# A layer with routed experts on one core: a multiplication moved to GpSimd, a third of the one-hot rows moved to VectorE, and the last block's stages scheduled earlier

## The chip, the core and the metric

The kernel runs on one core of a Trainium2 chip. The metric is device time in microseconds, the median of several executions. One execution is also profiled; the time of every instruction below comes from that one. PE is the TensorE matmul engine, DVE the VectorE, ACT the ScalarE, POOL the GpSimd, SP the SyncE, which issues most transfers.

## What is computed

One layer on 512 tokens of width 1024, all in float32: a norm and an input projection; eight heads of latent attention and eight heads of a chunked recurrence (RWKV-7); an output projection added to the input; then a layer of retrieved experts. That last part matters here:

```
q = (h @ w_pq) per head, two halves; s = q . sub_keys
s1, i1 = top_k(first half, 16);  s2, i2 = top_k(second half, 16)
top_s, pos = top_k(s1 + s2 over the 16 x 16 pairs, 16);  idx = i1 * 128 + i2 at pos
gate = softmax(top_s)
act = gelu(sum_d expert_u[idx] * h)
out += sum_k gate * act * expert_v[idx]        # 8 heads x 16 experts for each token
```

There are 128 x 128 = 16,384 experts, each a row of 1024 numbers in `expert_u` and in `expert_v`.

## The kernel before

The tokens are four blocks of 128. Each block passes through stages, written as generators: F (norm and projections of the recurrence, `front`), R (`chunks`), M (attention, `latent`), S (`scan`), B (output projection, norm, retrieval, `back`), and for the two dense blocks T (`routes`). B of block 3 also routes it. A loop at the end of the function picks, stage by stage, which generator emits its next piece, by a planner's estimate of costs.

The order in which instructions are emitted gives each a priority, earlier ones first. A scheduler then builds one fixed order for every engine's queue from these priorities and from its own model of durations; the chip follows this order, each queue strictly in turn. An instruction emitted inside `tc.high_priority(offset=4000)` counts as if it had been emitted 4000 instructions earlier. Before the change, only three helpers of the recurrence use it.

The experts are computed in two ways.

*Gathered rows*, for blocks 0 and 3 (`experts`): for each of the 128 picks of a token, POOL issues an indirect transfer of 128 rows from `expert_u` (L996), DVE multiplies it with h and sums (L1006); later the same for `expert_v`, which DVE adds into `acc` with the weight of each token (L1009). This makes 512 transfers of 128 x 1024 floats into four buffers (six in the early part). They are emitted after the stages, 96 steps of block 0 before the dense part and the rest after it, so the scheduler uses them to fill what is free.

*Dense*, for blocks 1 and 2 (`dense`): all 16,384 experts are computed for all 256 tokens, 128 groups of 128 experts. `up` multiplies a group of `expert_u` with h and applies gelu; `down` multiplies the result with the routing weights and with the group of `expert_v`, into four accumulators in PSUM. Most groups are split into a high and a low half first (L1094 on ACT, L1095 on DVE) and go as three products of halves.

The routing weights of the dense blocks are a matrix of tokens by experts, built by `make_gates` in 32 groups of eight tokens. `slots` holds, for each token (a column) and pick (a partition), the first index, the second index and the gate. For a group, B[pick, token, i] is 1 where i is the first index (L1061, DVE), times the gate (L1062, DVE); A[pick, token, j] is 1 where j is the second index, made on ACT as relu(1 - |j - index|) by eight Abs and one Relu (L1065, L1066). PE multiplies A and B token by token (L1074), and ACT evicts the products into `held` and `away` (L1077, L1078). B has two buffers, A has two, and the products have four banks of PSUM, which become the accumulators of `down` afterwards. The `away` part goes to DRAM and comes back later (L1080). The first 28 groups of `up` (L1133) are emitted before and between the groups of `make_gates`. Block 3's retrieval (L844, its top-16 lists L822 to L830) and routing share this stretch, since nothing in the dense part waits for them but the space they occupy.

Of the kernel before, what the change touches and what calls it, by code (L numbers as in the profile page):

```python
# [2 lines left out]

# [10 lines left out]
AF = mybir.ActivationFunctionType  # L14
OP = mybir.AluOpType
# [3 lines left out]
P = 128  # L19
D = 1024  # L20
S = 512
NB = S // P
# [8 lines left out]
URGENT = 4000  # L31
# [58 lines left out]
def layer_kernel(ctx: ExitStack, tc: tile.TileContext, x, pos, cvec, rvec, w_mla, w_rwkv, w_uq, w_ukv, lora, g2,  # L90
# [20 lines left out]
    mm, act, V, G = nc.tensor.matmul, nc.scalar.activation, nc.vector, nc.gpsimd  # L111
# [26 lines left out]
    def cst(shape, name, dt=F32, pool=pre):  # L138
        return pool.tile(shape, dt, name=name)
# [108 lines left out]
    iotap = cst([P, P], "iotap", pool=con)  # L248
# [14 lines left out]
    for j in range(16):  # L263
# [5 lines left out]
                    op=OP.mult)  # L269
# [26 lines left out]
    def bc(ap, n):  # L296
        return ap[:, :, None].to_broadcast([ap.shape[0], ap.shape[1], n])

    def bm(ap, n):
        return ap[:, None, :].to_broadcast([ap.shape[0], n, ap.shape[1]])  # L300
# [755 lines left out]
    def make_gates(dn, psd, held, far):  # L1056

        i1T, i2T, gT = slots
        for t0 in range(0, nd, 8):
            B = dn.tile([P, D], F32, tag="x", name=f"B{t0}", bufs=XB).rearrange("p (a b) -> p a b", a=8)  # L1060
            V.tensor_tensor(B, bm(iotap, 8), bc(i1T[:, t0:t0 + 8], P), op=OP.is_equal)  # L1061
            V.tensor_tensor(B, B, bc(gT[:, t0:t0 + 8], P), op=OP.mult)  # L1062
            A = dn.tile([P, 8, P], F32, tag="A", name=f"A{t0}", bufs=2)
            for j in range(8):
                act(A[:, j, :], iotap, AF.Abs, scale=-1.0, bias=i2T[:, t0 + j:t0 + j + 1])  # L1065
            act(A, A, AF.Relu, scale=-1.0, bias=1.0)  # L1066
            i = t0 % 16
            if i == 0:
                away = dn.tile([P, D], F32, tag="v", name=f"away{t0}", bufs=VB)
                away = away.rearrange("p (s t i) -> p s t i", s=P // SUB - HELD, i=SUB)  # L1070
            for h in range(2):
                p = psd.tile([P, 512], F32, tag="po", name=f"pg{t0}{h}", bufs=2 * len(DENSE))
                for j in range(4):
                    mm(p[:, j * P:(j + 1) * P], A[:, 4 * h + j, :], B[:, 4 * h + j, :], start=True, stop=True)  # L1074
                p4 = p.rearrange("p (t s i) -> p s t i", t=4, i=SUB)
                t = t0 + 4 * h
                act(held[:, :, t:t + 4, :], p4[:, :HELD], AF.Copy)  # L1077
                act(away[:, :, t % 16:t % 16 + 4, :], p4[:, HELD:], AF.Copy)  # L1078
            if i:
                nc.sync.dma_start(far[:, t0 // 16], away)  # L1080
            yield

    def dense():
# [110 lines left out]
        for i, _ in enumerate(make_gates(dn, psd, held, far)):  # L1194
            for e in range(FIRST + i * rest // n, FIRST + (i + 1) * rest // n):
                up(e, e >= AHEAD)
# [30 lines left out]
    running = [None] * len(lanes)  # L1227
    while any(lanes):
        best = None
        for i, todo in enumerate(lanes):  # L1230
            if not todo:
                continue
            t = at[i]
            if running[i] is None:
                deps = [d for b in todo[0][1] for d in after[todo[0][0]](b) if d[1] >= 0]
                if any(d not in done for d in deps):
                    continue
                t = max([t] + [done[d] for d in deps])
            if best is None or t < best[0]:
                best = (t, i)  # L1240
        t, i = best
        n, bs = lanes[i][0]
        fn, count, cost = stages[n]
        if running[i] is None:
            running[i] = fn(bs) if n == "B" else fn(*bs)
            at[i] = t
        lane[0] = LANE[n]
        try:
            next(running[i])
            at[i] += cost / count  # L1250
        except StopIteration:
            for b in bs:
                done[n, b] = at[i]
            lanes[i].pop(0)
            running[i] = None
# [67 lines left out]
```

## Time and profile before

| | |
|---|---|
| median of 3 executions | 1761.57 us (1759.91 to 1781.8) |
| the profiled execution | 1773.46 us, its span 1771.7 us |
| PE matmul, weight load | 1556.0 us (88%), 1319.3 us (74%) |
| DVE | 1358.6 us (77%) |
| ACT | 808.1 us (46%) |
| POOL | 777.8 us (44%), 512 of its instructions are gathers |
| moved by DMA | 537.52 MB, 303 GB/s; of it by the gathers 268.47 MB |
| mean granted TensorE clock | 0.926 of full speed |

The shares are averages over the whole span; the stages differ in what limits them. A window of the trace gives the busy time of each engine in one stretch, the granted clock, the mean busy share of the 16 DMA engines and the rate. Grouped lines give the work of one source line: how many instructions, how long in total, the mean, then how long the engine stood idle just before them and what ended that.

### The profile page before, as it was taken

How to read it: one execution, taken by the hardware profiler on the slowest of the kernel's cores; microseconds unless marked ns; L12 is line 12 of the kernel's file. 1: busy time of each engine (PE TensorE's matmuls, PEld its weight loads, DVE VectorE, ACT ScalarE, POOL GpSimd, SP SyncE). 2: the span in 40 equal slices, each digit the busy share in tenths (PEclk: the TensorE clock that was granted, in tenths of full speed). 3: DMA queues.
4: the chain of work that ended last, by engine and by line, in shares of the span. 5: the costliest groups of instructions: out<-in, count | busy, mean ns of one | idle time of the engine just before them, and what ended most of it. 6: DMA issues, size and time to landing. Idle time of an engine off the chain costs nothing. (4 is left out here: it accounts for less than half of the span.)

```text
span 1771.7 us, 29597 instructions
## 1 busy us (share of the span) xinstructions
PE 1556.0 (88%) x10803; PEld 1319.3 (74%) x10803; DVE 1358.6 (77%) x2788; ACT 808.1 (46%) x2007; POOL 777.8 (44%) x560
## 2 busy tenths in 40 slices
PE   7999998998799897789995668999969999899992
PEld 6896797876575686569985436788868888888872
DVE  3422435678886689988999857898879899898896
ACT  5645634455423422237798302444425444344440
POOL 1001100546674644454437644454445365464574
PEclk9999998998669889899997889999989999999997
DMA  8545644798889889889996899899999999999997
GB/s 279 187 140 189 228 160 129 273 362 275 300 303 385 297 312 322 311 319 359 377 308 209 314 318 347 335 360 345 350 324 367 347 334 364 348 350 364 331 340 274
DMA packets 165617, 537.52 MB, mean 303 GB/s; under 512 B 17824, under 2 KB 32800, under 8 KB 165472
## 3 DMA queue, kind: packets, MB, share of 16 engines
q0 software_dynamic: 73728, 268.47, 42.4%
q1 hardware_dynamic: 91744, 267.17, 42.2%
q8 instruction: 85, 1.39, 0.3%
q14 instruction: 60, 0.49, 0.1%
HBM read 517.34 MB, written 18.22 MB: 302 GB/s over the span
## 5 line engine op out<-in xcount | busy, mean ns | idle before, releaser
L996 POOL DMA_INDIRECT ga<-in_expert_v_dram,idx x235 | 375.8, 1599 | 315.5 <-DVE acc L1009 205.6
L996 POOL DMA_INDIRECT ga<-in_expert_u_dram,idx x225 | 287.5, 1278 | 312.8 <-DVE ga L1006 244.2
L1009 DVE SCALAR_TENSOR_TENSOR acc<-ga,dots,acc 128x1024 f32<-128x1024 f32 x235 | 300.5, 1279 | 33.3 <-DMA ga<-in_expert_v_dram,idx 32.8
L1006 DVE SCALAR_TENSOR_TENSOR ga<-ga,h 128x1024 f32<-128x1024 f32 x225 | 273.6, 1219 | 29.8 <-DMA ga<-in_expert_u_dram,idx 29.1
L1147 PE MATMUL ps<-dh,uh 128*128 128x256 f32 x800 | 231.7, 290 | 24.8 <-ACT uh L1094 24.8
L1147 PE MATMUL ps<-dh,ul 128*128 128x256 f32 x800 | 231.9, 290 | 13.4 <-DVE ul L1095 13.4
L1147 PE MATMUL ps<-dl,uh 128*128 128x256 f32 x800 | 230.5, 288 | 0.0
L1185 PE MATMUL po<-xh,t 128*128 128x512 f32 x544 | 186.1, 402 | 16.1 <-ACT xh L1094 16.1
L1147 PEld LDWEIGHTS ps<-dh,uh 128*128 128x128 f32 x800 | 157.0, 196 | 32.1 <-ACT uh L1094 27.4
L1147 PEld LDWEIGHTS ps<-dh,ul 128*128 128x128 f32 x800 | 156.7, 196 | 19.6 <-DVE ul L1095 17.1
L1147 PEld LDWEIGHTS ps<-dl,uh 128*128 128x128 f32 x800 | 156.8, 196 | 3.1 <-issue 0.5
L1185 PE MATMUL po<-x2h,t 128*128 128x512 f32 x408 | 135.3, 392 | 2.0 <-ACT x2h L1094 2.0
L1094 ACT ACTIVATE xh<-v 128x1024 fp32r<-128x1024 f32 x68 | 71.9, 1057 | 136.3 <-DMA v<-in_expert_v_dram 61.7
L1095 DVE TENSOR_TENSOR ul<-u,uh 128x1024 fp32r<-128x1024 f32 x100 | 121.9, 1220 | 13.6 <-ACT uh L1094 13.5
L1185 PEld LDWEIGHTS po<-xh,t 128*128 128x128 f32 x544 | 101.8, 192 | 39.6 <-ACT xh L1094 19.5
L844 PE MATMUL ps<-h2T,wst 128*128 128x128 f32 (+1 forms) x768 | 125.2, 319 | 4.2 <-DMA wst<-in_w_pq_dram 2.9
L1094 ACT ACTIVATE uh<-u 128x1024 fp32r<-128x1024 f32 x100 | 104.8, 1051 | 43.2 <-DMA u<-in_expert_ut_dram 33.2
L844 PEld LDWEIGHTS ps<-h2T,wst 128*128 128x128 f32 x768 | 110.8, 197 | 12.8 <-DMA wst<-in_w_pq_dram 2.2
L353 PE MATMUL ps<-hT,wst 128*128 128x129 f32 x896 | 110.8, 277 | 0.6 <-ACT t L311 0.6
L1185 PE MATMUL po<-xl,t 128*128 128x512 f32 x272 | 109.8, 404 | 0.7 <-DVE xl L1095 0.5
L1133 PE MATMUL ps<-t,u 128*128 128x256 f32 x448 | 108.0, 395 | 2.7 <-DMA u<-in_expert_ut_dram 2.0
L353 PEld LDWEIGHTS ps<-hT,wst 128*128 128x128 f32 x896 | 105.3, 191 | 6.3 <-issue 1.3
(423 smaller groups left out, 3132.6 us busy)
## 6 DMA issues: line engine op xcount, KB each, us to landing
u<-in_expert_ut_dram SPq DMA_DIRECT2D x128, 512.0 KB, 6.8
v<-in_expert_v_dram SPq DMA_DIRECT2D x128, 512.0 KB, 6.1
wst<-in_w_rwkv_dram SPq DMA_DIRECT2D x56, 512.0 KB, 4.4
wst<-in_w_pq_dram SPq DMA_DIRECT2D x48, 512.0 KB, 6.6
wst<-in_w_o_dram SPq DMA_DIRECT2D x24, 512.0 KB, 6.2
far<-away SPq DMA_DIRECT2D x16, 512.0 KB, 6.1
G<-far SPq DMA_DIRECT2D x16, 512.0 KB, 12.0
wst<-in_w_mla_dram SPq DMA_DIRECT2D x16, 336.0 KB, 6.5
```

What stands on the lines that cost most here:

```text
L353: mm(p[:, :P + 1], w[:, kc, :], hT[:, kc, :], start=kc == 0, stop=kc == KC - 1)
L844: mm(p[:, :nb * P], w[:, kc, :], h2T[:, kc, :], start=kc == 0, stop=kc == KC - 1)
L996: G.indirect_dma_start(out=t, out_offset=None, in_=table, in_offset=bass.IndirectOffsetOnAxis(ap=idx[:, j:j + 1], axis=0))
L1006: V.scalar_tensor_tensor(u, u, 1.0, h2, op0=OP.mult, op1=OP.mult, accum_out=dots[:, j:j + 1])
L1009: V.scalar_tensor_tensor(acc, row_of(expert_v, j), dots[:, j:j + 1], acc, op0=OP.mult, op1=OP.add)
L1094: act(hi, t, AF.Copy)
L1095: V.tensor_tensor(lo, t, hi, op=OP.subtract)
L1133: mm(p, u[:, kc, :], hd[kc // 2][:, kc % 2, :], start=kc == 0, stop=kc == KC - 1)
L1147: mm(p, a[:, k, :], h[:, kc, :], start=kc + i == 0, stop=kc == KC - 1 and i == 2)
L1185: mm(po[i][n], ww[:, i * P:(i + 1) * P], vv[:, cols], start=e + k == 0, stop=e == P - 1 and k == 2)
```

## The change

It has three parts. In `make_gates` the multiplication of B with the gate is issued on GpSimd instead of VectorE. Of each three groups the third gets its A from one comparison on VectorE instead of the nine operations on ScalarE; that is ten of the 32. And block 3's stages M, S and B are emitted inside `tc.high_priority(offset=4000)`.

```
-            V.tensor_tensor(B, B, bc(gT[:, t0:t0 + 8], P), op=OP.mult)
+            G.tensor_tensor(B, B, bc(gT[:, t0:t0 + 8], P), op=OP.mult)
             A = dn.tile([P, 8, P], F32, tag="A", name=f"A{t0}", bufs=2)
-            for j in range(8):
-                act(A[:, j, :], iotap, AF.Abs, scale=-1.0, bias=i2T[:, t0 + j:t0 + j + 1])
-            act(A, A, AF.Relu, scale=-1.0, bias=1.0)
+            if t0 // 8 % 3 == 2:
+                V.tensor_tensor(A, bm(iotap, 8), bc(i2T[:, t0:t0 + 8], P), op=OP.is_equal)
+            else:
+                for j in range(8):
+                    act(A[:, j, :], iotap, AF.Abs, scale=-1.0, bias=i2T[:, t0 + j:t0 + j + 1])
+                act(A, A, AF.Relu, scale=-1.0, bias=1.0)
...
         try:
-            next(running[i])
+
+            with tc.high_priority(offset=URGENT) if bs == (NB - 1,) and n in "MSB" else nullcontext():
+                next(running[i])
             at[i] += cost / count
```

## Rows read from the trace of the kernel before

**Rows 1.** Windows: stretch, its length, busy us (instructions) by engine, clock, DMA share, GB/s.

```profile
core 0: us, PE busy (x) PEld busy (x) DVE busy (x) ACT busy (x) POOL busy (x), PEclk, DMA share, GB/s
...
700.00:792.00 92.00, 69.27 (x313) 50.41 (x313) 85.09 (x363) 20.61 (x53) 44.90 (x36) 0.87 0.87 316
792.00:989.00 197.00, 174.17 (x1178) 161.32 (x1176) 184.85 (x395) 162.78 (x472) 99.52 (x59) 0.93 0.88 313
989.00:1050.00 61.00, 33.91 (x82) 18.51 (x83) 40.08 (x68) 7.45 (x13) 28.83 (x17) 0.80 0.89 322
1050.00:1742.00 692.00, 639.97 (x3771) 557.82 (x3770) 611.00 (x778) 288.46 (x428) 352.85 (x231) 0.97 0.95 346
1742.00:1771.70 29.70, 0.43 (x2) 0.00 (x0) 16.67 (x16) 0.00 (x0) 10.65 (x9) 0.57 0.71 244
```

**Rows 2.** The last link of the chain of waits: start, duration, what.

```profile
1766.50 1.28 DVE acc L1009
```

**Rows 3.** Groups of ACT, 792 to 989 us: count, busy, mean ns, idle before.

```profile
L1065 ACT ACTIVATE A<-iotap,slots 128x128 f32<-128x128 f32 x256 | 78.9, 406 | 0.0
L1066 ACT ACTIVATE A<-A 128x1024 f32<-128x1024 f32 x32 | 33.9, 1064 | 0.1
...
L1077 ACT ACTIVATE G<-pg 128x256 f32<-128x256 f32 x64 | 24.6, 384 | 19.5 <-PE pg L1074 19.5
```

**Rows 4.** Groups of PE, 792 to 989 us.

```profile
L1074 PE MATMUL pg<-B,A 128*128 128x128 f32 x512 | 71.7, 298 | 10.3 <-DVE B L1062 4.3 <-ACT A L1066 4.0 <-DVE B L1061 2.1
...
L844 PE MATMUL ps<-h2T,wst 128*128 128x128 f32 x256 | 30.9, 275 | 0.0
```

**Rows 5.** Groups of DVE, 792 to 989 us.

```profile
L1009 DVE SCALAR_TENSOR_TENSOR acc<-ga,dots,acc 128x1024 f32<-128x1024 f32 x44 | 56.1, 1274 | 2.9 <-DMA ga<-in_expert_v_dram,idx 2.9
...
L1062 DVE TENSOR_TENSOR B<-B,slots 128x1024 f32<-128x1024 f32 x32 | 38.7, 1213 | 0.1
L1006 DVE SCALAR_TENSOR_TENSOR ga<-ga,h 128x1024 f32<-128x1024 f32 x15 | 18.3, 1218 | 2.2 <-DMA ga<-in_expert_u_dram,idx 2.1
...
L830 DVE FIND_INDEX8 ti<-tv,t 128x8 uint32<-128x128 f32 x16 | 4.4, 285 | 0.0
...
L822 DVE MAX8 tv<-t 128x8 f32<-128x128 f32 x16 | 3.5, 278 | 0.0
```

**Rows 6.** B's comparison by line: min/median/max ns, first and last start.

```profile
L1061 DVE TENSOR_TENSOR B<-iotap,slots x32: 1198/1212/1237, 791.8 to 981.3; 128x1024 f32<-128x1024 f32 x32
```

**Rows 7.** GpSimd's memsets by line, the same columns.

```profile
L616 POOL MEMSET t<- x8: 515/532/544, 42.5 to 467.5; 64x512 f32 x8
```

**Rows 8.** Groups of POOL, 792 to 989 us.

```profile
L996 POOL DMA_INDIRECT ga<-in_expert_v_dram,idx x46 | 83.4, 1813 | 76.0 <-DVE acc L1009 47.2 <-DVE ga L1006 4.8 <-DVE ti L877 3.6
L996 POOL DMA_INDIRECT ga<-in_expert_u_dram,idx x13 | 16.1, 1239 | 20.9 <-DVE ga L1006 9.2 <-DVE ti L824 4.7 <-DMA ga<-in_expert_v_dram,idx 3.4
```

**Rows 9.** Waits, 792 to 989 us: total us, times, longest.

```profile
POOL ga L996 <- DVE acc L1009: 47.2, 28, 4.9
```

**Rows 10.** A power of 128x1 on POOL by line: min/median/max ns.

```profile
L306 POOL TENSOR_TENSOR nfr<-nfv,mhalf x4: 557/990/1475, 192.6 to 774.4; 128x1 f32<-128x1 f32 x4
```

**Rows 11.** POOL in order of time: start, duration, what.

```profile
575.37 1.48 POOL L306 TENSOR_TENSOR nfr<-nfv,mhalf 128x1 f32<-128x1 f32 x1 [3.00 <-DVE nfv L304]
...
990.96 10.59 POOL L996 DMA_INDIRECT ga<-in_expert_u_dram,idx  x1 [0.65 <-DVE acc L1009]
```

**Rows 12.** DVE in order of time, beside these.

```profile
575.20 1.21 DVE L1006 SCALAR_TENSOR_TENSOR gx<-gx,h 128x1024 f32<-128x1024 f32 x1
...
993.62 3.08 DVE L1164 TENSOR_TENSOR wst<-wst,G 128x256 f32<-128x256 f32 x6
```

**Rows 13.** By line from 700 us on: block 3's output projection, its retrieval; slots.

```profile
L787 PE MATMUL ps<-wst,yT x32: 592/592/697, 727.0 to 769.2; 128*128 128x512 f32 x32
...
L844 PE MATMUL ps<-h2T,wst x256: 272/275/275, 799.2 to 879.4; 128*128 128x128 f32 x128
...
L978 ACT ACTIVATE slots<-ps x6: 257/275/283, 772.9 to 793.8; 128x128 f32<-128x128 f32 x6
```

**Rows 14.** Waits of SP's queue, 700 to 1050 us: total us, times, longest.

```profile
SPq L293 <- PE ps L844: 24.2, 10, 4.1
```

More of the change, by code (lines that the diff above doesn't have):

```diff
@@ L1 @@
 import math
-from contextlib import ExitStack
+from contextlib import ExitStack, nullcontext
 import concourse.bass as bass
```

## The prediction

> **What bounds the kernel now.** I read the stage table first [rows 1]: busy time of each engine between the points where the work changes. The reader should see three regimes. From 792 to 989 us the routing matrix is built: DVE is busy 184.85 of 197 us, PE 174.17, ACT 162.78. From 1050 to 1742 us the dense pass runs: the DMA engines are busy 0.95 of the time at 346 GB/s, PE 639.97 of 692 us. Between them lies a hole (989 to 1050) in which PE works 33.91 of 61 us. PE has nothing left after 1742 us (0.43 us), and the chain of waits ends in an accumulation of a gathered row at 1766.5 us [rows 2]. So the dense pass and the gathered rows share the DMA engines to the end, and every gather put off from an earlier stage is paid there: a gather moves 128 rows of 1024 floats, 0.524 MB, which is 1.5 us at 346 GB/s.
>
> Then the groups inside the build. On ACT the Abs, the Relu and two groups of evictions of about 24.6 us each are nearly all of the work, and ACT's largest idle time, 19.5 us, is for products of PE [rows 3]; PE's products wait 10.3 us for A and B [rows 4]. ACT with that wait is 182 of 197 us: the loop through ACT paces the build. DVE is as full, but 74.4 us of it (56.1 + 18.3) are gathered rows, which nothing in the build waits for [rows 5]. Thus less work on ACT shortens the build; less on DVE mainly makes room for gathers.
>
> **The change, part by part.** *The multiplication leaves DVE*: 32 of 1.213 us, 38.7 us [rows 5]. *The one-hot rows of ten groups* (2, 5, ... 29 of 32) go from ACT to DVE: ACT loses 10/32 of 78.9 + 33.9 = 35.3 us [rows 3], DVE gains ten comparisons of B's shape, 10 x 1.212 = 12.1 us [rows 6]. DVE: -26.6 us.
>
> *The multiplication on GpSimd*, 128x1024, has no row. Nearest is a memset that writes 512 columns in 0.532 us [rows 7]: 1.06 us for 1024 if its reads hide behind its writes, 3.2 us if two reads and a write go one after the other. I take the middle, 2.1 us: 67 us on POOL beside 99.5 us of gather issues [rows 8], 167 of 197 us. The Trainium skill (GPSIMD Engine Reference, 3.1) states 4497 ns for an addition twice as wide; an estimate from it is 2.25 us, 72 us in all, and the sum would not move.
>
> The multiplication now stands in POOL's order behind gathers that wait for a buffer, up to 4.9 us each [rows 9]; behind it wait the next gather and the products of its group. B has two buffers and a group takes 197/32 = 6.2 us; comparison, multiplication and products need 1.2 + 2.1 + 2.2 us (71.7/32, [rows 4]), which leaves 6.9 us of 12.3. So I cost this wait at nothing; without that cover, one late multiplication of 10 us costs some 3 us.
>
> *What the multiplication costs DVE* is the disputed term. GpSimd's tiny operation takes 0.56 us at best and 1.48 us when it starts inside a gathered-row instruction of DVE, ending about 0.4 us after that one [rows 10 to 12]. A gather issue stood 10.59 us while DVE ran short two-input instructions with no gap [rows 11, 12]. So DVE makes GpSimd wait. The reverse shows nowhere, but GpSimd read at most 8 columns at a time in this kernel. The hold on DVE is between 0 and the whole multiplication, at most 3.2 us; the rows show DVE keeping its place, so I take 0.6 us, 19 us in all. DVE's net is -7 us.
>
> *The build after that*: ACT 127 us, or 147 with its wait for products; DVE without gathers 184.85 - 74.4 - 7 = 103; PE still 174. PE is next in line, so the build ends 197 - 174 = 23 us earlier. In those 23 us 23/197 x 59 = 7 gathers [rows 8] are not issued and come later, 7 x 1.5 = 10.6 us. Net -12.4 us.
>
> *Block 3's last stages* (attention, scan, output projection, retrieval, routing) go 4000 instructions forward. Before, block 3's output projection ran within 727 to 769 us and its retrieval matmuls at 799 to 879 us, while the dense blocks' lists (slots) were complete at 794 us [rows 13]. So block 3 was behind the dense blocks' routing and beside the build. Put ahead, it takes out of the build 30.9 us of PE [rows 4] and on DVE five groups of list operations (4.4 to 3.5 us, 20 us) and smaller ones, some 30 us [rows 5]. With these go its SyncE loads (8 of w_o, 16 of w_pq, 4 of keys), past the dense blocks' loads and the first expert loads; the weight queue already waited 24.2 us for block 3's matmuls to free a buffer [rows 14]. On POOL its small powers (0.56 to 2.5 us each) pass gathers. What it pays depends on where it lands. PE was idle 22.73 us of 700 to 792: at best it fills that. At worst the dense blocks' routing, and the build with it, starts later by all 30.9 us of PE and gets nothing back. Taken work out of one stage and put into the stage before it, with idle time for most of it and a chain in front that waits for it: I take 0 and keep -22.7 and +30.9 for the range.
>
> **Sum.** The profiled execution took 1773.5 us (span 1771.7), 11.9 above the median of 1761.6. 1773.5 - 12.4 = 1761.1; against the median, 1749 us. This case alone spans 1739 (no gather put off) to 1762 (all of it paid back). A difference under 2%, 35 us, can't be told from none here: below 1726 is faster, above 1797 slower.
>
> **Rivals.**
>
> *The hold (slower).* Place: 792 to 989 us, DVE. If the multiplication keeps DVE out for its whole length, 32 x 2.1 = 67 us come against 26.6 saved: +40.6, of which DVE's 12.2 us of idle time take some. 28.4 us remain, 23 gathered rows of 1.25 us, put off at 1.5 us each: +35, 1797 us; at 3.2 us each, +77, 1838. It costs from a hold of (26.6 + 12.2)/32 = 1.2 us on, and passes 2% at 2.1 us. For: both sides stay nearly full, and POOL waits for DVE in the rows. Against: B's 32 comparisons, in a stretch where POOL is busy half of the time, all last 1198 to 1237 ns [rows 6].
> The Trainium skill (SBUF — State Buffer, "Who interferes with whom") says that a VectorE instruction with two SBUF inputs and a GpSimd instruction that reads SBUF exclude each other for the whole instruction, whichever started first. By that rule this rival decides. The trace agrees for one direction (1.48 against 0.56 us); no run here yet shows the other.
>
> *Block 3 fills the holes (faster).* With its lists done early, 22.7 us of PE's idle time before 792 go: 12.4 + 22.7 = 35, 1726 us. If the space that block 3's pools hold is free early enough for the dense pass to start without the hole of 989 to 1050 (27.1 us of PE idle), 1699. Middle: 1713 us. For: PE idles in both places. Against: in both the DMA engines are at 0.87 and 0.89, so there is little room to load ahead.
>
> *Paid back, or no effect.* Every us won in the build returns as gathers on the DMA engines, and block 3's stages can't move because their tiles wait for block 2's: 1762 us. For: the dense pass at 0.95.
>
> **Chances and range.** Forecast 0.38, paid back 0.17, holes filled 0.25, hold 0.20. Below 1726: 0.20 of the third and 0.06 of the first's tail together with block 3's gain, 0.26. Above 1797: 0.12 of the hold, 0.05 for block 3 delaying the build, 0.17. Between: 0.57. Range 1702 to 1800: the deep end of the holes (under 0.1) and the upper half of the hold (about 0.1) are left out.
>
> **What would show it.** After the change the 32 multiplications stand on POOL at 1.06 to 3.2 us; longer means that they wait inside. DVE's two-input instructions beside them at 1.2 us and without gaps: no hold; gaps of 1 to 2 us in front of them, named after nothing or POOL: hold. ACT in the build about 127 us, the build some 174 us long with PE as its fullest engine. Gathers before the dense pass fewer by about 7, dense pass at 346 GB/s as before. Block 3's retrieval matmuls before the slots are written, and the slots no later than 794 us: step right; slots at 815 or later: block 3 delays the build. Wrong altogether I would be if the dense pass itself changed its length by more than 20 us, since nothing in my sum acts there except gathers.

## The result, and the profile after

The changed kernel takes 1795.0 us (median of 4 runs), the kernel before 1763.5 in the same comparison. The ratio is 1.0137, 95% interval 1.009 to 1.0183; this ratio and those below are taken over the fast runs of each comparison and need not be the quotient of the two medians, which is 1.0179 here. The loss is clear of its interval, but under the 2% from which the prediction would have called the kernel slower. The forecast of 1749 us had the wrong sign; that 1795 lies inside the range of 1702 to 1800 is no merit of the sum, which had the kernel 12 us faster. The profiled execution took 1795.96 us, its span is 1794.2.

The stage table of the changed kernel, as in [rows 1], cut where its own build begins and ends:

```profile
core 0: us, PE busy (x) PEld busy (x) DVE busy (x) ACT busy (x) POOL busy (x), PEclk, DMA share, GB/s
700.00:810.00 110.00, 81.64 (x383) 60.53 (x382) 94.56 (x377) 26.84 (x68) 52.05 (x44) 0.83 0.87 312
810.00:1023.00 213.00, 181.87 (x1172) 167.54 (x1172) 197.57 (x359) 133.89 (x385) 143.32 (x84) 0.90 0.78 272
1023.00:1050.00 27.00, 12.97 (x33) 7.36 (x32) 21.39 (x40) 5.87 (x10) 7.22 (x6) 0.70 0.88 320
1050.00:1775.00 725.00, 670.78 (x3829) 577.20 (x3828) 630.99 (x803) 289.96 (x430) 352.42 (x240) 0.97 0.94 343
1775.00:1794.20 19.20, 0.99 (x5) 0.46 (x3) 11.32 (x12) 0.00 (x0) 4.67 (x4) 0.66 0.71 254
```

Read by the first comparison of B, the last product of a one-hot pair and the last matmul, the two spans divide like this:

| us | before | after | difference |
|---|---|---|---|
| build begins | 791.8 | 809.6 | +17.8 |
| build | 196.5 | 212.1 | +15.6 |
| dense pass to its last matmul | 754.1 | 754.3 | +0.2 |
| tail behind it | 29.3 | 18.2 | -11.1 |

So the run lost 33 us ahead of the dense pass and got 11 back in the tail. ACT did lose its work, 162.8 to 133.9 us, and nothing became shorter for it.

The groups of the changed kernel between 810 and 1023 us, DVE, ACT, PE and POOL (count, busy, mean ns, idle before), answering to [rows 3 to 6] and [rows 8]:

```profile
L1009 DVE SCALAR_TENSOR_TENSOR acc<-ga,dots,acc 128x1024 f32<-128x1024 f32 x41 | 75.9, 1851 | 5.3 <-DMA ga<-in_expert_v_dram,idx 5.1
L1061 DVE TENSOR_TENSOR B<-iotap,slots 128x1024 f32<-128x1024 f32 x32 | 45.1, 1414 | 1.2 <-PE ps L958 1.0 <-PE pg L1077 0.2
L1006 DVE SCALAR_TENSOR_TENSOR ga<-ga,h 128x1024 f32<-128x1024 f32 x11 | 18.9, 1723 | 6.1 <-DMA ga<-in_expert_u_dram,idx 6.1
L1065 DVE TENSOR_TENSOR A<-iotap,slots 128x1024 f32<-128x1024 f32 x10 | 13.8, 1382 | 0.0
...
L1080 ACT ACTIVATE G<-pg 128x256 f32<-128x256 f32 x64 | 24.7, 386 | 45.2 <-PE pg L1077 45.0
...
L1077 PE MATMUL pg<-B,A 128*128 128x128 f32 x512 | 76.0, 307 | 18.3 <-POOL B L1062 16.8 <-ACT A L1069 1.5
...
L1062 POOL TENSOR_TENSOR B<-B,slots 128x1024 f32<-128x1024 f32 x32 | 74.4, 2330 | 24.3 <-DVE B L1061 24.1
```

The means of DVE are the finding. A gathered row's accumulation takes 1851 ns instead of 1274, its dot product 1723 instead of 1218, a comparison 1414 instead of 1212. Without these three lines and the multiplication DVE's busy time in its build was 184.4 - 74.4 - 38.8 - 38.7 = 32.5 us before and is 197.6 - 94.8 - 45.1 - 13.8 = 43.9 now, for 265 small operations instead of 272. Stretching in all: 41 x 0.577 + 11 x 0.505 + 32 x 0.202 + 10 x 0.17 + 11.4 = 48.8 us, 1.5 us for each of the 32 multiplications. Where it lies shows in order of time (start, duration; POOL and DVE of the changed kernel, 857 to 873 us):

```profile
857.71 1.89 POOL L1062 TENSOR_TENSOR B<-B,slots 128x1024 f32<-128x1024 f32 x1 [0.53 <-DVE B L1061]
857.82 2.87 DVE L1009 SCALAR_TENSOR_TENSOR acc<-ga,dots,acc 128x1024 f32<-128x1024 f32 x1
...
862.70 2.02 POOL L1062 TENSOR_TENSOR B<-B,slots 128x1024 f32<-128x1024 f32 x1
...
863.26 1.50 DVE L1015 TENSOR_TENSOR dots<-dots,gate 128x32 f32<-128x32 f32 x1 [0.30 <-ACT dots L1014]
...
866.77 2.01 POOL L1062 TENSOR_TENSOR B<-B,slots 128x1024 f32<-128x1024 f32 x1
866.95 5.55 DVE L1009 SCALAR_TENSOR_TENSOR acc<-ga,dots,acc 128x1024 f32<-128x1024 f32 x3
```

Each of these stretched DVE instructions begins just behind the start of a multiplication and ends after it: 2.87 us begun at 857.82 ends 1.1 us after POOL at 859.60, so its own 1.27 us were hardly begun while POOL worked. A product of 128x32 takes 1.50 us. The wait is inside the instruction; no gap and no wait's name shows it.

Block 3's part shows in the line that writes the dense blocks' lists, at 793.8 us before [rows 13]:

```profile
L978 ACT ACTIVATE slots<-ps x6: 272/282/296, 797.2 to 815.8; 128x128 f32<-128x128 f32 x6
```

### The profile page after: what moved, and what is told of

The parts are those of the page before. It is cut to its first block, busy times and chain, and to the rows that moved or that the text cites. A ratio compares the mean times of both kernels' runs of the same rounds, so it can differ in the third digit from the quotient of the medians.

```text
span 1794.2 us, 29558 instructions
## 1 busy us (share of the span) xinstructions
PE 1583.2 (88%) x10803; PEld 1336.5 (74%) x10803; DVE 1383.5 (77%) x2766; ACT 780.7 (44%) x1919; POOL 811.7 (45%) x592
## 4 chain that ended last, share of the span: by engine, by line
PE 41%; issue 17%; DVE 14%; DMA 14%; POOL 10%; ACT 2%; SPq 0%; POOLq 0%; DVEq 0%; ACTq 0%
POOL ga L996 9%; PE po L1188 7%; PE ps L1150 7%; DMA ga<-in_expert_v_dram,idx 5%; PE ps L353 5%; PE ps L844 4%; DVE acc L1009 4%; DMA ga<-in_expert_u_dram,idx 3%; PE ps L669 3%; DVE ga L1006 2%; DMA v<-in_expert_v_dram 2%; PE ps L787 2%; PE ps L364 1%; DVE B L1061 1%; PE ps L1136 1%
## 5 line engine op out<-in xcount | busy, mean ns | idle before, releaser
L996 POOL DMA_INDIRECT ga<-in_expert_v_dram,idx x235 | 350.6, 1492 | 350.5 <-DVE acc L1009 223.1
L996 POOL DMA_INDIRECT ga<-in_expert_u_dram,idx x225 | 273.4, 1215 | 256.0 <-DVE ga L1006 182.3
L1009 DVE SCALAR_TENSOR_TENSOR acc<-ga,dots,acc 128x1024 f32<-128x1024 f32 x235 | 324.4, 1380 | 31.5 <-DMA ga<-in_expert_v_dram,idx 30.7
L1006 DVE SCALAR_TENSOR_TENSOR ga<-ga,h 128x1024 f32<-128x1024 f32 x225 | 279.0, 1244 | 46.0 <-DMA ga<-in_expert_u_dram,idx 45.7
L1150 PEld LDWEIGHTS ps<-dh,ul 128*128 128x128 f32 x800 | 160.3, 201 | 15.6 <-DVE ul L1098 13.5
L1097 ACT ACTIVATE xh<-v 128x1024 fp32r<-128x1024 f32 x68 | 72.0, 1058 | 120.4 <-DMA v<-in_expert_v_dram 58.7
L1097 ACT ACTIVATE uh<-u 128x1024 fp32r<-128x1024 f32 x100 | 104.5, 1050 | 24.6 <-DMA u<-in_expert_ut_dram 15.2
```

The costliest lines, as they stand in the source:

```text
L996: G.indirect_dma_start(out=t, out_offset=None, in_=table, in_offset=bass.IndirectOffsetOnAxis(ap=idx[:, j:j + 1], axis=0))
L1006: V.scalar_tensor_tensor(u, u, 1.0, h2, op0=OP.mult, op1=OP.mult, accum_out=dots[:, j:j + 1])
L1009: V.scalar_tensor_tensor(acc, row_of(expert_v, j), dots[:, j:j + 1], acc, op0=OP.mult, op1=OP.add)
L1097: act(hi, t, AF.Copy)
L1150: mm(p, a[:, k, :], h[:, kc, :], start=kc + i == 0, stop=kc == KC - 1 and i == 2)
```

## The experiments

All ratios are to the kernel before as it ran in the same comparison.

| kernel | ratio | 95% | build, us | tail, us |
|---|---|---|---|---|
| before | 1 | | 791.8 to 988.3 | 29.3 |
| the change | 1.0137 | 1.009 to 1.0183 | 809.6 to 1021.7 | 18.2 |
| e1 multiplication alone | 1.0096 | 1.0059 to 1.0134 | 791.0 to 1022.8 | 18.4 |
| e2 third A alone | 1.0017 | 0.9996 to 1.0038 | 788.7 to 987.9 | 32.5 |
| e3 priority alone | 1.0024 | 1.0006 to 1.0043 | 810.0 to 1009.9 | 5.5 |
| e4 multiplication, third A | 1.0155 | 1.0118 to 1.0192 | 784.0 to 998.0 | 33.2 |
| e7 third A, priority | 1.0082 | 1.0052 to 1.0112 | 817.1 to 1021.7 | 6.8 |
| e6 writes for the multiplication | 0.9988 | 0.996 to 1.0015 | 784.7 to 972.6 | 41.2 |
| e8 B in one step on DVE | 0.9916 | 0.9892 to 0.994 | 782.7 to 976.2 | 38.6 |
| e12 e8 and third A | 1.0054 | 1.0027 to 1.0081 | 788.1 to 970.0 | 58.7 |

**The three parts alone, and in pairs.** The multiplication (e1):

```diff
-            V.tensor_tensor(B, B, bc(gT[:, t0:t0 + 8], P), op=OP.mult)
+            G.tensor_tensor(B, B, bc(gT[:, t0:t0 + 8], P), op=OP.mult)
```

> The kernel before with the multiplication on GpSimd alone. Hold theory: DVE's two-input instructions beside the 32 multiplications grow from 1.21 and 1.27 us to 2 us or more, together some 40 us, so the build is about 15 us longer than the 197 us of before and starts where it did (792 us); the run is 10 to 25 us slower than before. Schedule theory (the whole loss is block 3's priority): the build starts at 792 us and takes 197 us or less; the run is within 8 us of before.

Measured 1.0096. DVE's groups in its build (791 to 1022.8 us):

```profile
L1009 DVE SCALAR_TENSOR_TENSOR acc<-ga,dots,acc 128x1024 f32<-128x1024 f32 x48 | 79.3, 1652 | 6.8 <-DMA ga<-in_expert_v_dram,idx 6.3
L1061 DVE TENSOR_TENSOR B<-iotap,slots 128x1024 f32<-128x1024 f32 x32 | 42.0, 1319 | 4.5 <-PE pg L1074 3.3 <-PE ps L922 1.2
L1006 DVE SCALAR_TENSOR_TENSOR ga<-ga,h 128x1024 f32<-128x1024 f32 x19 | 34.6, 1822 | 15.1 <-DMA ga<-in_expert_u_dram,idx 15.0
```

The same stretching with neither of the other parts, and of the three parts alone the dearest, 17 us. The build is 35 us longer, not the 15 expected, but it holds 66 gathers instead of 59, and the dense pass and the tail are 9 and 11 us shorter.

The third A (e2):

```diff
-            for j in range(8):
-                act(A[:, j, :], iotap, AF.Abs, ...)
-            act(A, A, AF.Relu, scale=-1.0, bias=1.0)
+            if t0 // 8 % 3 == 2:
+                V.tensor_tensor(A, bm(iotap, 8), bc(i2T[:, t0:t0 + 8], P), op=OP.is_equal)
+            else:
+                ... (the lines as before)
```

> The kernel before with only every third group's A made by one VectorE comparison. If ACT paces the build, ACT loses 35 us of 163 and the build ends 10 to 23 us earlier than 989 us; the run is 0 to 15 us faster. If DVE paces it (10 more instructions of 1.2 us on an engine with 12 us of idle time), the build ends up to 12 us later and the run is 0 to 12 us slower.

Measured 1.0017, and the build 199.2 us, as the theory had it by which DVE paces it. Its stage row, columns as in the stage table:

```profile
788.70:987.90 199.20, 173.59 (x1175) 161.07 (x1174) 191.75 (x402) 133.21 (x380) 110.23 (x56) 0.94 0.84 303
```

ACT gave up 29 us and the build did not become shorter, with 55 gathers in it instead of 59; DVE went from 184 to 192. So ACT alone does not pace the build.

The priority (e3):

```diff
-            next(running[i])
+            with tc.high_priority(offset=URGENT) if bs == (NB - 1,) and n in "MSB" else nullcontext():
+                next(running[i])
```

> The kernel before with only block 3's stages 4000 ahead. Schedule theory: slots are complete near 816 us instead of 794, the build starts and ends about 18 us later, and the run is 15 to 25 us slower. Hold theory (all of the loss is the multiplication's): slots at 794 us, the run within 8 us of before. My recorded forecast took 0, with -23 and +31 as bounds.

Measured 1.0024: the slots came as the schedule theory said (816.2 us), the time as the other. The build begins 18 us later, and the tail is 24 us shorter: 210 instead of 197 gathers are issued ahead of the build.

The pairs put the lines of two of these diffs together, e4 the first two, e7 the last two:

```diff
+ e4: lines of e1 and e2
+ e7: lines of e2 and e3
```

> The change without block 3's priority. Hold theory: build starts at 792 us, DVE's instructions stretched by about 40 us in all, PE waits 40 us for the multiplication; 5 to 20 us slower than before. Schedule theory: without the priority the rest of the change gains what was forecast, some 12 us faster than before, build 174 us long.

> The whole change with the multiplication back on VectorE. If the multiplication is what costs, this is within 10 us of before (0 to 10 us slower: 3 us of each of the other two parts measured alone) and 20 us faster than the whole change. If the three parts hurt one another, it stays 15 us or more slower than before.

e4 lost more than the 20 us that the hold theory allowed. e7 lies between its two cases, 15 us slower than before and 10, not 20, faster than the whole change.

The three parts alone sum to 0.96 + 0.17 + 0.24 = 1.37%, the change's own 1.37%, but that is in part luck. Both pairs cost more than their parts, 1.55 against 1.13% (e4) and 0.82 against 0.41% (e7): each sum lies just outside the pair's interval, and is hardly told from it once the intervals of the parts are counted too. The multiplication costs 17 us alone (e1), 24 beside the third A (1.0155 against 1.0017), and 10 in the change itself (1.0137 against e7's 1.0082). So its share of the change's loss is not one number, and what the third A and the priority cost together no run explains. No part gains anything.

**The multiplication by itself (e5).** A kernel with nothing of the layer in it, all sections kept apart:

```diff
+        two_in(8)                    # DVE: product of two tiles, 128x1024
+        mult(8)                      # POOL alone
+        two_in(24); mult(8)          # both
+        32 x DVE 128x512 with one input in PSUM; mult(8)
+        24 x DVE tensor_scalar, one input; mult(8)
+        two_in(24); 12 x POOL memset
+        128 x DVE tensor_scalar 128x128, is_equal and mult
```

> The two instructions by themselves, in sections parted by barriers (nothing of the layer is computed): 8 DVE products of two SBUF tensors 128x1024 alone; 8 GpSimd multiplications of the change's shape alone; 24 of the former beside 8 of the latter; 32 DVE products 128x512 with one input in PSUM beside 8; 24 one-input DVE instructions 128x1024 beside 8; 24 two-input products beside 12 GpSimd memsets; 128 DVE instructions 128x128 that compare and multiply at once. Hold theory: alone 1.2 and 1.9 us; together the two-input section takes the sum of both, about 24 x 1.14 + 8 x 1.9 = 43 us, single products lasting 3 us; the one with PSUM and the one with memsets are not stretched. Queue theory (GpSimd is only late, DVE is not held): the two-input section takes 27 to 30 us.

In order of time (start, duration of the whole run of instructions):

```profile
9.36 9.18 DVE L38 TENSOR_TENSOR vo<-t,t 128x1024 f32<-128x1024 f32 x8 [3.31 <-SPq L41]
18.72 14.87 POOL L34 TENSOR_TENSOR B<-t,g 128x1024 f32<-128x1024 f32 x8 [18.28 <-SPq L41]
33.74 40.94 DVE L38 TENSOR_TENSOR vo<-t,t 128x1024 f32<-128x1024 f32 x24 [15.20 <-SPq L41]
33.78 22.79 POOL L34 TENSOR_TENSOR B<-t,g 128x1024 f32<-128x1024 f32 x8 [0.19 <-SPq L41]
74.80 19.23 DVE L52 TENSOR_TENSOR vo<-ps,t 128x512 f32<-128x512 f32 x32
74.84 14.88 POOL L34 TENSOR_TENSOR B<-t,g 128x1024 f32<-128x1024 f32 x8 [18.28 <-SPq L41]
94.16 28.14 DVE L56 TENSOR_SCALAR vo<-t 128x1024 f32<-128x1024 f32 x24
94.20 18.52 POOL L34 TENSOR_TENSOR B<-t,g 128x1024 f32<-128x1024 f32 x8 [4.47 <-SPq L41]
122.42 27.34 DVE L38 TENSOR_TENSOR vo<-t,t 128x1024 f32<-128x1024 f32 x24
122.44 10.78 POOL L61 MEMSET B<- 128x1024 f32 x12 [9.72 <-SPq L41]
149.90 32.89 DVE L64 TENSOR_SCALAR vo<-t,g 128x128 f32<-128x128 f32 x128
```

Alone a product takes 9.18 / 8 = 1.15 us and the multiplication 14.87 / 8 = 1.86 us. Beside 8 multiplications, 24 products of two SBUF tiles take 40.94 us against 27.34 beside memsets, which leave them at their length alone (1.14 us each): 1.7 us for each multiplication, nearly its whole length. 27.34 + 14.87 = 42.2 is close to 40.94: the two take turns. With one input in PSUM neither is stretched. The Trainium skill (SBUF — State Buffer, "Who interferes with whom") says just this: a VectorE instruction with two SBUF inputs contends with a GpSimd instruction that reads SBUF, not with one that only writes it. These rows agree in both points.

One input in SBUF does not make an instruction free, though. The 24 one-input instructions take 28.14 us, and POOL's 8 multiplications 18.52 instead of 14.87. By duration (min/median/max ns) of the former:

```profile
L56 DVE TENSOR_SCALAR vo<-t x24: 677/680/2386, 94.2 to 121.6; 128x1024 f32<-128x1024 f32 x24
```

Eight of them take 2.4 us, one beside each multiplication, and the rest 0.68. Why these are held and the products with PSUM are not, no run here tells.

**Writes in place of the multiplication (e6),** with the third A and without the priority. POOL writes B twice, which takes as long as a multiplication alone (0.95 us each) and reads nothing; the gates are left out:

```diff
-            V.tensor_tensor(B, B, bc(gT[:, t0:t0 + 8], P), op=OP.mult)
+            for _ in range(2):
+                G.memset(B, 0.0625)
```

> The change without block 3's priority (as the earlier run of that), but each multiplication on GpSimd is two memsets of B, which write and read nothing: the gate is left out of the result, and about the same time, 2.1 us, stays on POOL's queue with the same place in the order. Hold theory: DVE's instructions return to 1.21 and 1.28 us, the build falls from 214 us to 200 or less, and the run is 10 to 25 us faster than with the multiplication, 0 to 8 us slower than before. Queue theory (POOL's order and its waits cost, not the hold): the build stays above 208 us and the run stays 20 us or more slower than before.

Measured 0.9988, where e4, with the multiplication in their place, is at 1.0155: the hold and what follows from it are worth 1.7%, 29 us. The builds of e4 (784 to 998 us) and, in the second fence, of e6 (785 to 973 us): the stage row, DVE's row accumulation, and PE's wait for B.

```profile
784.00:998.10 214.10, 177.12 (x1164) 164.57 (x1163) 195.34 (x369) 133.38 (x381) 164.91 (x87) 0.90 0.78 278
...
L1009 DVE SCALAR_TENSOR_TENSOR acc<-ga,dots,acc 128x1024 f32<-128x1024 f32 x41 | 70.2, 1712 | 2.7 <-DMA ga<-in_expert_v_dram,idx 2.6
...
L1077 PE MATMUL pg<-B,A 128*128 128x128 f32 x512 | 74.5, 304 | 25.7 <-POOL B L1062 25.7
```

```profile
784.70:972.60 187.90, 167.21 (x1178) 157.16 (x1176) 157.25 (x371) 133.29 (x382) 141.97 (x121) 0.95 0.88 317
...
L1009 DVE SCALAR_TENSOR_TENSOR acc<-ga,dots,acc 128x1024 f32<-128x1024 f32 x42 | 53.6, 1276 | 5.5 <-DMA ga<-in_expert_v_dram,idx 5.2 <-DVE ga L1006 0.3
...
L1078 PE MATMUL pg<-B,A 128*128 128x128 f32 x512 | 68.8, 291 | 14.5 <-POOL B L1063 13.9 <-issue 0.5
```

1276 ns: no stretching. ACT's work is the same in both, 55 and 56 gathers are issued in them, and POOL's step stands at the same place in the order; DVE is busy 157 instead of 195 us and the build is 26 us shorter. What lengthens the build is the hold. The granted clock, a mean over stretches at 1.2 and at 2.4 GHz, is 0.95 in e6's build and 0.90 in e4's, where PE stands longer for B; how much of the 29 us this makes is not told apart.

PE's products wait 13.9 us for POOL here, 25.7 in e4 and 16.8 in the change. That is not yet a price of POOL's order: with the multiplication on DVE they wait nearly as long for it, 15.0 us in e2 (and 20.9 in e7, against 16.8 in the change).

```profile
L1077 PE MATMUL pg<-B,A 128*128 128x128 f32 x512 | 72.8, 301 | 21.2 <-DVE B L1062 15.0 <-ACT A L1069 6.1
```

e6 against e2 also shows what relief of DVE does by itself: ACT's work is the same, the gathers in the build nearly so (56 and 55), DVE is busy 157 instead of 192 us, and the build is 11 us shorter. Yet the run gains nothing against before: the build is 9 us shorter, and the tail, with 14 gathers instead of 8, 12 us longer.

**B in one step on DVE (e8).** The opposite of the change: comparison and gate in one instruction for each of the 8 rows, GpSimd not used.

```diff
-            V.tensor_tensor(B, bm(iotap, 8), bc(i1T[:, t0:t0 + 8], P), op=OP.is_equal)
-            V.tensor_tensor(B, B, bc(gT[:, t0:t0 + 8], P), op=OP.mult)
+            for j in range(8):
+                V.tensor_scalar(B[:, j, :], iotap, i1T[:, t0 + j:t0 + j + 1], gT[:, t0 + j:t0 + j + 1],
+                                op0=OP.is_equal, op1=OP.mult)
```

> The kernel before with B made on VectorE by eight instructions of 128x128, each comparing with the first index of one token and multiplying by its gate, in place of the two of 128x1024; nothing on GpSimd, A as before. Such instructions (one input) were about 0.14 us apart on DVE, so 32 x (2.28 - 1.1) = 38 us of DVE go. If DVE paces the build, it ends 15 to 30 us earlier than 989 us and the run is 8 to 25 us faster. If ACT paces it (my forecast's reading), build and run stay within 5 us of before.

Measured 0.9916: it beats both kernels, 1754.0 us against 1767.0 before. One step takes 0.257 us in e5 (32.89 / 128), not the expected 0.14; 8 of them take 2.06 us, against 1.21 + 1.21. In the build they save 77.5 - 70.1 us:

```profile
L1062 DVE TENSOR_SCALAR B<-iotap,slots,slots 128x128 f32<-128x128 f32 x256 | 70.1, 352 | 4.1 <-PE pg L1075 4.0
```

DVE is busy 177.3 instead of 184.4 us there. The build is only 3 us shorter, not the 15 to 30 of the one theory, and the run gains more than the 5 us of the other: 19 us in the profiled spans, 13 by the medians. Of the 19, 9 lie ahead of the build and are no gain of the edit: up to there the ten profiled kernels without a priority run the same instructions in the same order on each engine (a handful of neighbouring records aside), and their builds begin anywhere between 782.2 us (e15) and 796.2 (e13). 16 are a shorter dense pass, and the tail gives 9 back. The dense pass starts earlier: block 3's list of picks is done at 939.8 us instead of 964.2, and the dense pass's first split product begins at 943.2 instead of 968.7. These two lines (min/median/max ns, first and last start), before and, in the second fence, e8:

```profile
L971 ACT ACTIVATE idx<-ps x2: 267/272/277, 322.5 to 964.2; 128x128 int32<-128x128 f32 x2
...
L1147 PE MATMUL ps<-dh,uh x800: 274/283/681, 968.7 to 1693.4; 128*128 128x256 f32 x160
```

```profile
L971 ACT ACTIVATE idx<-ps x2: 277/277/277, 320.2 to 939.8; 128x128 int32<-128x128 f32 x2
...
L1148 PE MATMUL ps<-dh,uh x800: 274/283/682, 943.2 to 1662.9; 128*128 128x256 f32 x160
```

In the changed kernel the two stand at 1007.6 and 1013.3, in e2 at 956.2 and 959.7, in e12 at 948.8 and 952.1: the split products always begin 3 to 6 us behind block 3's list, and over all sixteen profiles of the layer the last matmul comes 761 to 789 us behind that. That block 3's tiles must be free first fits the code, but no run moved this link by itself.

**Which stage of block 3 delays the build (e9 to e11).** The priority for one stage at a time (the line as in the change, and what replaces it):

```diff
-            with tc.high_priority(offset=URGENT) if bs == (NB - 1,) and n in "MSB" else nullcontext():
+            with tc.high_priority(offset=URGENT) if bs == (NB - 1,) and n == "M" else nullcontext():   # "S", "B"
```

> The kernel before, with block 3's attention (M) alone a priority of 4000 ahead. Theory 1 (the attention's loads and matmuls take block 2's place in the queues): the dense blocks' slots are written at 810 to 818 us, as with all three stages ahead (816.2), against 793.8 before, and the time is 1.000 to 1.005 of before. Theory 2 (the scan does it): slots at 790 to 797 us. Theory 3 (output projection, retrieval and routing do it): slots at 790 to 797 us too, and the runs with those stages alone tell 2 from 3.

> The kernel before, with block 3's scan (S) alone a priority of 4000 ahead. Theory 1: slots at 790 to 797 us, the time within 0.3% of before. Theory 2 (the scan's chain of DVE work pushes block 2's attention and output projection back): slots at 805 us or later. Theory 3: as theory 1.

> The kernel before, with block 3's output projection, retrieval and routing (B) alone a priority of 4000 ahead. Theory 3 (these stages stand in front of the dense blocks' routing): slots at 805 us or later, since block 3's 30.9 us of retrieval matmuls come first on PE. Theories 1 and 2: slots at 790 to 797 us, since these stages still wait for an attention and a scan that keep their old place; the time within 0.3% of before.

Measured 1.0013 (0.9985 to 1.004), 1.0056 (1.0025 to 1.0086) and 1.0069 (1.0039 to 1.0098); the lists are written at 801.4, 812.6 and 826.8 us. No single theory holds: each stage by itself delays them, B, the last in the block's order, the most. M's delay is hardly clear of the spread, since without a priority the lists are written between 783.9 and 797.9 us, and its time is not shown to differ from before. The delay is there long before block 3's own work. Stage rows of before and of e10, then PE's 64x64 products of the recurrence between 510 and 540 us, before and e10:

```profile
520.00:540.00 20.00, 16.67 (x131) 10.99 (x127) 12.90 (x18) 4.61 (x10) 11.07 (x10) 1.00 1.00 377
...
L669 PE MATMUL ps<-t,t 64*64 64x64 f32 x106 | 6.4, 261 | 0.0
L669 PE MATMUL ps<-t,INT 64*64 64x64 f32 x64 | 5.4, 244 | 1.2 <-ACT t L684 1.2
```

```profile
520.00:540.00 20.00, 19.21 (x213) 17.30 (x214) 18.37 (x29) 9.09 (x22) 16.43 (x14) 0.63 0.90 314
...
L669 PE MATMUL ps<-t,t 64*64 64x64 f32 x183 | 15.3, 313 | 3.0 <-DVE t L677 2.9
L669 PE MATMUL ps<-t,INT 64*64 64x64 f32 x96 | 9.9, 288 | 0.0
```

With a stage put ahead the scheduler packs the recurrence's small products there, 279 instead of 170, and the granted clock, in both kernels at its lower level (0.50, 1.2 GHz) from 500 to 510 us, comes back to the upper one between 530 and 540 instead of at 520. The six kernels with a priority show 0.50 between 520 and 530 us, the ten others 0.83 to 1.00. In those six the order of PE and ACT differs from before's from 372 us on, and from 540 us on output projections and block 3's attention are behind before's by 12 to 29 us. Why the scheduler's order changes so far ahead of the work that was put ahead stays open.

**Where the gain of a shorter build goes (e12 to e15).** e12 takes e8 and the third A together; e13, e14 and e15 leave out block 3's last 14 gathered rows from before, e12 and e8:

```diff
-                if g:
+                if g and not (b == GATHERED[-1] and g == ng and i >= GROUP - 14):
                     j = (g - 1) * GROUP + i
```

> The kernel before with the comparison and the multiplication of B done together by VectorE, 8 instructions of 128 columns for a group, and every third group's other one-hot rows by VectorE too; GpSimd does neither. Theory 'VectorE paces the build' (the fused form alone gave 0.9916): the ten comparisons give 12 us back to VectorE, and the time is 0.993 to 1.000 of before, no better than the fused form alone. Theory 'ACT is next once VectorE is relieved': 35 us less on ACT shortens the build further, and the time is 0.980 to 0.989.

Measured 1.0054, neither theory: the build is the shortest of all and the run slower. Its row in the build and its tail (1717.8 to 1776.6 us), DVE and POOL:

```profile
788.10:970.00 181.90, 167.65 (x1177) 158.19 (x1175) 171.93 (x583) 132.29 (x381) 59.65 (x46) 0.95 0.85 299
...
L1009 DVE SCALAR_TENSOR_TENSOR acc<-ga,dots,acc 128x1024 f32<-128x1024 f32 x28 | 36.0, 1286 | 18.0 <-DMA ga<-in_expert_v_dram,idx 17.8
L996 POOL DMA_INDIRECT ga<-in_expert_v_dram,idx x24 | 28.0, 1166 | 21.1 <-DVE acc L1009 12.3 <-DMA ga<-in_expert_v_dram,idx 6.7 <-issue 2.1
```

The scheduler put 45 gathers into this build instead of 59, and through the dense pass as many as before; 24 are left behind the last matmul instead of 8, and the tail is 58.7 us instead of 29.3: 29.4 / 16 = 1.8 us for each. DVE is busy 0.95 of this build, 0.94 before and 0.96 in e2, but 0.92 in e8 and 0.84 in e6: most builds are nearly as long as DVE's work in them, rows included, but DVE is not the only limit. Whether ACT was next after e8 stays open, since this build also holds 13 gathers fewer than e8's.

> The kernel before with block 3's last 14 gathered rows of expert_v left out (gather and accumulation). It prices a gathered row that is left for the end: in the trace of before 8 gathers are issued after the last matmul and the tail is 29.3 us. Theory 'a row put off is paid for at the end, after the matmuls': the tail falls to 8 to 14 us and the time by 15 to 21 us, 0.988 to 0.992 of before. Theory 'the dense pass ends the run, the rows only ride along in its shadow': under 5 us, 0.997 or more.

> The kernel in which VectorE makes B in one step and every third A (1.0054 of before, build 181.9 us against 196.5, but 45 gathers in it against 59 and 24 after the last matmul against 8), with the same 14 rows left out. Theory 'its shorter build was paid back as rows put off': the time falls by 14 rows of 1.7 to 2.1 us, 24 to 29 us, to 0.989 to 0.992 of before, and the tail from 58.7 to 30 to 35 us. Theory 'the loss lies in the dense pass, which starts before its loads are there': it falls by less than 10 us, to 1.000 or more.

> The kernel in which VectorE makes B in one step (0.9916 of before, 13 gathers after the last matmul, tail 38.6 us), with the same 14 rows left out. If rows put off are paid at 1.7 to 2.1 us each also here: the time falls by 22 to 28 us, to 0.976 to 0.979 of before, tail 11 to 17 us. If its gain lies in fewer rows at the end: it comes out level with the kernel before with the same cut, 0.988 to 0.992.

Measured 0.9893 (0.9851 to 0.9936), 0.9894 (0.9836 to 0.9951) and 0.9792 (0.9745 to 0.9838); tails 6.3, 31.1 and 10.8 us. Taking 14 rows off the end gives before 19 us, e12 28 us (1.0054 to 0.9894) and e8 22 us, with dense passes that keep their length within 4 us. Per row this is 1.4 us in before, where 8 gathers stood behind the last matmul, 1.6 in e8 with 13, and 28 / 14 = 2.0 in e12 with 24: what its build saves is paid back there. e13 and e14 came as 'a row put off is paid for at the end' had it, e15 within 0.1% of that. e14 still has 10 gathers behind its last matmul and e13 none: its tail is 25 us longer, which takes back most of the 18 and 9 us by which its build and dense pass are shorter, and the two come out level. e15 against e13 (0.9792 against 0.9893) repeats e8's gain: 1.0%, again with a dense pass of 738 us where before's has 754 and e13's 758.

## Why the prediction was wrong, step by step

- *"The loop through ACT paces the build"*: wrong, and the step that made the forecast faster. Busy time plus one wait was taken for the limit, and DVE's rows for work "which nothing in the build waits for". In DVE's fixed order the rows stand between the comparisons, so a comparison behind a row waits for it; no run took the rows alone out of the build. e2 takes 29 us off ACT and the build is 2.7 us longer, not 23 shorter. e6 takes 35 us off DVE from there, and it is 11 us shorter with one gather more in it, against "less on DVE mainly makes room for gathers". Even so it comes to 187.9 us, not 174.
- *The multiplication's length*: taken 2.1 us, measured 1.86 alone, 2.33 in the kernel. Right.
- *"I take 0.6 us"* for the hold on DVE: wrong size, 1.5 us in the kernel and 1.7 in e5. DVE's net was forecast at -26.6 + 19 = -7 us; it is -26.6 + 48.8 = +22, less 7 rows that moved out, and DVE's busy time rose by 13.2 us, the build by 15.6. The argument against the rival, comparisons of 1198 to 1237 ns beside a POOL busy half of the time [rows 6], looked at gather issues and not at an instruction that reads two operands from SBUF.
- *"So I cost this wait at nothing"*: not shown wrong. PE's products waited 16.8 us for B in the change, more than the 6.4 before [rows 4], so two buffers did not cover it; but with the same other parts and the multiplication on DVE they wait 20.9 (e7), and without the hold 13.9 on POOL against 15.0 on DVE (e6, e2). Only with the hold and without the priority is the wait longer on POOL, 25.7 against 15.0 (e4, e2) and 23.1 against 6.4 (e1, before).
- *Block 3's priority, 0 with -22.7 and +30.9*: the sign given by its own test, "slots at 815 or later: block 3 delays the build", is what came (815.8), but not by block 3's retrieval matmuls standing in front; they are at 819 us and later in e3 too, still beside the build. What delays the build instead stays open. Alone the start moved by 18 us and the run by 0.24%; 13 more gathers were issued ahead of the build, and the tail gave 24 us back.
- *Gathers put off*: forecast 7 fewer in the build, and it is 7 (52), which is luck: the build is longer, not shorter, and none were put off, since 262 instead of 256 were issued before the dense pass. The price of 1.5 us by bandwidth lies between the 1.4 and 2.0 us by which a row left out shortened the run (e13 to e15); behind the last matmul, where each waits for a buffer and a transfer, it is low (1.8 to 2.0 us in e12).
- *The rivals*: the hold is the mechanism that came. Its price of +35 us at a hold of 2.1 us assumed that DVE's 12.2 us of idle time take some of it; at 1.5 us it would have given 32 x 1.5 - 38.8 = 9 us, 7 rows, +11. The multiplication alone cost 17 us with the idle time still there. "Paid back" is what e6 and e12 show; in e2 the build won nothing that could be paid back.

## What to carry to other kernels

When DVE is the fuller engine, a two-operand elementwise step moved to GpSimd can be paid for on DVE almost in full (1.7 us of 1.86 in e5, 1.5 in the kernel, for the 1.21 that it saves there); look for a fused form on DVE first (e8). Do not strike background work off the list of what paces a stage when it stands in the same in-order queue: count it with its stage. And where work is interleaved through the whole run by a fixed order, a shorter stage holds less of it, so look at what is left behind the last matmul before claiming a gain.

## What the runs showed of the hardware that was not expected

Two engines that exclude each other show it as longer instructions, not as gaps or waits: a product of 128x32 stood 1.50 us, and three accumulations 5.55. GpSimd's memset of 128x1024, 0.95 us, does not do this to DVE, and neither does the multiplication to a DVE instruction with one input in PSUM (32 in 19.23 us, 0.60 each). An instruction with a single SBUF input was held all the same, 2.39 us instead of 0.68, and each multiplication beside it took 2.3 us (18.52 / 8) instead of 1.86. A fused comparison and multiplication of 128x128 costs 0.257 us in a row of 128, so eight are 0.85 of the two wide instructions that they replace.
